# Block sums of the up-projection weights, made in the prompt's pass and stored for the sample's

## The chip, the core and the metric

The kernel runs on one core of a Trainium2 chip. The metric is device time in microseconds (us); lower is better. The core's engines run side by side, each with its own queue of instructions: TensorE (PE, matmuls; PEld its weight loads), VectorE (DVE), ScalarE (ACT), GpSimd (POOL) and SyncE (SP, which issues most DMAs). GpSimd issues DMAs too, from a queue of its own. Operands lie in SBUF, an on-chip memory of 128 partitions; matmuls accumulate into PSUM, which has eight banks of 128 x 512 fp32.

## The reference

One layer of an encoder is applied with the same weights to a prompt of 512 tokens and then to a sample of 1024 tokens, all in fp32, model width 1024. A retention branch and a latent-attention branch are merged by gates and projected (`w_out`); then follows the gated MLP that the change is about:

```python
    x = x + merged @ w_out[l]
    h = rms_norm(x, g_ffn[l])
    u = depthwise_conv3(h @ w_up[l], conv_w[l], conv_b[l])
    x = x + (jax.nn.silu(u[..., :D_FF]) * u[..., D_FF:]) @ w_down[l]
```

`w_up` is 1024 x 5632 and `w_down` 2816 x 1024. `depthwise_conv3` mixes each token with its two neighbours, channel by channel.

## The kernel before

**Precision.** An fp32 product is made of three products of a shorter type: `split` writes `hi` (a rounded copy, ScalarE, L121) and `lo` (source minus `hi`, VectorE, L122), and the matmuls hi x hi, hi x lo and lo x hi add up in PSUM. Every weight block is loaded (`raw`, 512 KB), split into `whi` and `wlo`, and used. Tensors are kept transposed, channels on partitions and tokens along the row, in 128-channel pieces.

**Order.** The layer function does the prompt, then the sample. A scheduler with a timeline of its own lays the instructions of each engine into one queue, so an engine does them in that order and waits at the first that isn't ready. Tiles come from pools; a tile tag with n buffers makes the next use wait until the n-th last one is read out.

**Prompt MLP** (L520 to L637). `psw` is the projection by `w_out`; its result is added to x, scaled to h2 and split (`h2h`, `h2l`), and x goes to DRAM. `do_up(j)` makes the 128 channels j of both halves of the up projection (`psu`, 48 matmuls), scales by the norm (`rb2`), applies the convolution (one ScalarE pass L579, two VectorE passes L580 and L581 for a half), silu and the gate product, and splits the result (`gh`, `gl`). `do_down(i)` takes two such blocks through `w_down`: eight matmul groups `psd` of 6, each added to y (L614). Up and down blocks alternate, and pieces of the sample's input preparation (`prep`: x loads, `hh`/`hl` splits, squares) run in between, with the norm of the sample's input (`rstd_n`, `spread`) at the end. The sample's projections `psc` follow.

**Sample MLP** (`mlp_by_seven`, L643 on). The up projection is done by a scheme of seven products on 2 x 2 blocks instead of eight. Its data units are b11, t2, t3 (pool "far") and t1, b21, t4, b22 (pool "near"), made of sums of quarters of h2. Its weight units, for each of 22 pairs j of column blocks, are the quarters a11, a12, a22 and the sums s1 = a21 + a22, s2 = s1 - a11, s3 = a11 - a21, s4 = a12 - s2. `up_weights(j)` loads the two 512 KB blocks of the pair, makes the four sums on GpSimd (L689 to L694) and splits the seven 512-wide units. `up_pair(j)` runs the seven products (12 matmuls each) in the order b11, t2, t3, t1, b21, t4, b22 into the tiles `psxw` (X and W), `psy`, `psz`, then combines them (L786 to L793, three of the sums on GpSimd), scales by `rb`, convolves (L797 to L799) and stores the gated result to DRAM (`gact`, L803). The near units are built at the start of the stage from VectorE splits and GpSimd sums. The norm of h2 (`pn_n`, `psr_n`) is computed in pair 0, after all its products. The down projection (`psd`, L836) follows as a stage of its own.

Of the kernel before, what the change touches and what calls it, by code (L numbers as in the profile page):

```python
# [45 lines left out]
def encoder(ctx: ExitStack, tc: tile.TileContext, a: dict):  # L46
# [226 lines left out]
    def layer(L, yT, following=None):  # L273
# [19 lines left out]
        def dense(ps, w, xh, xl):  # L293
            kn = len(xh)
            for k in range(kn):
                for pi, (wk, x) in enumerate(((w[k][0], xh), (w[k][0], xl), (w[k][1], xh))):
                    for h in range(nh):
                        nc.tensor.matmul(  # L298
                            ps[h] if isinstance(ps, list) else ps[:, hs[h]], wk, x[k][:, hs[h]],
                            start=(k == 0 and pi == 0), stop=(k == kn - 1 and pi == 2))  # L300

# [18 lines left out]
        for j in range(6):  # L320
# [177 lines left out]

        mgp, mgst = open_pool(f"md{sq}")
# [20 lines left out]
        hp2, h2st = open_pool(f"h2{sq}", 1, "right")  # L520
        h2h, h2l = new_split(hp2, KD, "h2")
        rb2 = hp2.tile([P, s], F32, tag="rb2", name=f"rb2{sq}")
        xp, xst = open_pool(f"xo{sq}", 2, "right")
        acc = xp.tile([P, s], F32, tag="acc", name=f"acc2{sq}", bufs=1)
        for m in range(KD):
            w = load_k(a["wout"][m], KD, P)
            x = xp.tile([P, s], F32, tag="x", name=f"xo{m}{sq}")
            nc.sync.dma_start(x, xT[m])
            ps = acc_tile(f"psw{m}{sq}")
            dense(ps, w, mh, ml)  # L530
            g = gffn[:, m:m + 1]
            nc.vector.tensor_tensor(x, ps[:, :s], x, op=ALU.add)
# [811 lines left out]
```

## Time and profile before

| | |
|---|---|
| Runs | 2975.9, 2975.2 and 3527.12 us; median 2975.9 |
| Profiled execution | 2975.95 us; its span 2974.2 us |
| TensorE busy in the span | 2905.5 us (98%) |
| VectorE, ScalarE, GpSimd busy | 67%, 45%, 20% |
| DMA | 323.89 MB, mean 109 GB/s |
| Prompt's `psw`, MLP and the sample's `psc` and first norm | 537.3 to 1028.1 us of the span |
| Sample's up projection | 2246.9 to 2728.7 us of the span |

A row of the profile names line, engine and operation, then what is written and what is read (`out<-in`, buffer numbers left out), the shape and the count; behind the bar stand busy time and mean ns of one. PEclk is the clock granted to TensorE as a share of full speed. "Idle before, releaser" tells how long the engine stood still ahead of an instruction and what ended the wait. The busy time of neighbouring instructions of one engine can overlap a little: a matmul of 512 columns is listed with some 0.39 us, while its successor starts 0.23 us after it, so the pace of TensorE is read from starts (in the chain of waits: so many matmuls in so many us) and not from its mean duration.

### The profile page before, as it was taken

The page shows a single profiled execution, that of the slowest core. Times are in us where ns is not written, and L with a number is a line of the kernel's source. Part 1 is how long each engine was busy: PE and PEld are TensorE (multiplying, and loading weights), DVE is VectorE, ACT ScalarE, POOL GpSimd, SP SyncE. Part 2 cuts the span into 40 slices and gives each one's busy share as a digit, 9 for nine tenths or more (in the row PEclk, how much of TensorE's full clock was granted, in tenths as well). Part 3 has the DMA queues.
Part 4 walks back from the last instruction along what each step waited for, and adds up shares of the span by engine and source line. Part 5 has one row for each costly group of instructions (what it writes and reads, how often), then busy time and mean ns, then how long its engine had stood idle before and what let it go on. Part 6 is the DMA issues. An engine that isn't in the chain of part 4 may idle for free.

```text
span 2974.2 us, 41678 instructions
## 1 busy us (share of the span) xinstructions
PE 2905.5 (98%) x15720; PEld 2499.0 (84%) x15720; DVE 1992.4 (67%) x3602; ACT 1340.4 (45%) x2634; POOL 592.6 (20%) x540
## 2 busy tenths in 40 slices
PE   8999999999999999999999999999998999999999
PEld 7998887878887899999888888888886777777887
DVE  6766786578666446765347888872458999988343
ACT  5554674344332234444246677651234444434222
POOL 1011220000000001001122122100025667764000
PEclk9999999999999999999999999999998999999999
DMA  6225444543232411112332222324431212224463
GB/s 192 84 92 180 141 143 148 181 142 121 92 99 89 156 44 44 54 45 77 114 108 73 73 78 79 121 83 169 143 134 50 85 64 85 71 78 163 144 204 113
DMA packets 127801, 323.89 MB, mean 109 GB/s; under 512 B 13040, under 2 KB 45680, under 8 KB 127600
## 3 DMA queue, kind: packets, MB, share of 16 engines
q1 hardware_dynamic: 78192, 232.60, 24.2%
q0 software_dynamic: 49408, 88.62, 9.7%
q8 instruction: 124, 2.03, 0.3%
q14 instruction: 77, 0.63, 0.1%
HBM read 257.73 MB, written 63.44 MB: 108 GB/s over the span
## 4 chain that ended last, share of the span: by engine, by line
PE 81%; DVE 12%; ACT 2%; issue 2%; POOL 2%; DMA 2%; SPq 0%; DVEq 0%; POOLq 0%; ACTq 0%
PE psr L890 14%; PE psd L836 8%; PE S L1185 6%; PE pv L1218 4%; DVE wu L122 3%; PE pq L1131 2%; PE pkv L1062 2%; PE psw L298 2%; DVE t L798 2%; DVE t L799 2%; PE pt L1206 2%; PE psxw L761 2%; PE po L1010 2%; POOL u L791 1%; PE psz L761 1%
## 5 line engine op out<-in xcount | busy, mean ns | idle before, releaser
L121 ACT ACTIVATE whi<-raw 128x1024 fp32r<-128x1024 f32 (+3 forms) x274 | 263.9, 966 | 670.4 <-PE psd L836 144.6
L122 DVE TENSOR_TENSOR wlo<-raw,whi 128x1024 fp32r<-128x1024 f32 (+2 forms) x272 | 301.4, 1110 | 224.5 <-ACT whi L121 224.4
L122 DVE TENSOR_TENSOR ptl<-pt,pth 128x512 fp32r<-128x512 f32 x160 | 107.3, 685 | 26.2 <-ACT pth L121 24.9
L836 PE MATMUL psd<-gh,whi 128*128 128x512 f32 x352 | 109.4, 394 | 4.1 <-ACT gh L121 4.1
L1187 DVE TENSOR_REDUCE mx<-S 128x1 f32<-128x1024 f32 (+1 forms) x96 | 99.9, 1041 | 14.7 <-PE S L1185 13.6
L836 PE MATMUL psd<-gl,whi 128*128 128x512 f32 x352 | 108.8, 389 | 0.0
L836 PE MATMUL psd<-gh,wlo 128*128 128x512 f32 x352 | 108.5, 389 | 0.0
L1190 ACT ACTIVATE pe<-S,mx,qsc 128x1024 f32<-128x1024 f32 (+1 forms) x96 | 102.4, 1067 | 6.6 <-DVE mx L1188 6.5
L121 ACT ACTIVATE pth<-pt 128x512 fp32r<-128x512 f32 x160 | 91.2, 599 | 29.8 <-PE pt L1206 28.0
L798 DVE SCALAR_TENSOR_TENSOR t<-u,consts,t 128x1023 f32<-128x1023 f32 x44 | 78.4, 1795 | 25.7 <-ACT t L797 25.1
L121 ACT ACTIVATE wu<-s 128x512 fp32r<-128x512 f32 x88 | 53.4, 626 | 82.2 <-POOL s L690 63.0
L1206 PE MATMUL pt<-ident,pe 128*128 128x128 f32 x640 | 89.0, 273 | 0.5 <-DVE pe L1192 0.2
L797 ACT ACTIVATE t<-u,consts 128x1024 f32<-128x1024 f32 x44 | 53.6, 1244 | 76.7 <-POOL u L791 59.6
L122 DVE TENSOR_TENSOR wu<-s,wu 128x512 fp32r<-128x512 f32 x88 | 82.9, 964 | 1.7 <-ACT wu L121 1.5
L1131 PE MATMUL pq<-whi,qc 128*128 128x384 f32 x288 | 83.7, 346 | 0.0
L122 DVE TENSOR_TENSOR wu<-rawu,wu 128x512 fp32r<-128x512 f32 x66 | 80.0, 1213 | 4.1 <-ACT wu L121 4.0
L1017 POOL TENSOR_TENSOR rsd<-rsd,mhalf 128x2 f32<-128x2 f32 x24 | 20.0, 832 | 314.2 <-DVE rsd L1016 314.2
L836 PEld LDWEIGHTS psd<-gh,whi 128*128 128x128 f32 x352 | 67.0, 191 | 18.5 <-ACT gh L121 4.5
L1206 PEld LDWEIGHTS pt<-ident,pe 128*128 128x128 f32 x640 | 73.9, 140 | 7.2 <-DVE ptl L122 1.3
L799 DVE SCALAR_TENSOR_TENSOR t<-u,consts,t 128x1023 f32<-128x1023 f32 x44 | 78.1, 1777 | 0.0
L836 PEld LDWEIGHTS psd<-gl,whi 128*128 128x128 f32 x352 | 66.1, 188 | 13.7
L836 PEld LDWEIGHTS psd<-gh,wlo 128*128 128x128 f32 x352 | 66.1, 188 | 13.7
(7524 smaller groups left out, 9908.1 us busy)
## 6 DMA issues: line engine op xcount, KB each, us to landing
raw<-wr SPq DMA_DIRECT2D x48, 512.0 KB, 3.5
raw<-wup SPq DMA_DIRECT2D x44, 512.0 KB, 3.5
rawu<-wup SPq DMA_DIRECT2D x44, 512.0 KB, 3.5
gr<-gact SPq DMA_DIRECT2D x44, 512.0 KB, 3.5
raw<-wg SPq DMA_DIRECT2D x32, 512.0 KB, 4.0
qc<-c0s POOLq DMA_DIRECT2D x16, 768.0 KB, 5.6
raw<-wdn SPq DMA_DIRECT2D x22, 512.0 KB, 3.6
gact<-t POOLq DMA_DIRECT2D x22, 512.0 KB, 3.1
```

Source lines behind the costliest of these rows:

```text
L121: first = nc.scalar.activation(hi, src, AF.Copy)
L122: nc.vector.tensor_tensor(lo, src, hi.bitcast(F32), op=ALU.subtract)
L798: nc.vector.scalar_tensor_tensor(t[:, 1:], u[i][:, :s - 1], convw[:, 0, c:c + 1], t[:, 1:], op0=ALU.mult, op1=ALU.add)
L799: nc.vector.scalar_tensor_tensor(t[:, :s - 1], u[i][:, 1:], convw[:, 2, c:c + 1], t[:, :s - 1], op0=ALU.mult, op1=ALU.add)
L836: nc.tensor.matmul(acc_[i][h], w[:, ms], x[:, t_of[h]], start=(k == 0 and pi == 0), stop=(k == NF - 1 and pi == 2))
L890: nc.tensor.matmul(ps[:, t], x[k][:, tk], w, start=(k == 0 and pi == 0), stop=(k == KD - 1 and pi == 2))
L1131: nc.tensor.matmul(ps[:, :384], x[:, k, tk], w, start=(k == 0 and pi == 0), stop=(k == 2 and pi == 2))
L1185: nc.tensor.matmul(S[:, ks], l_, r_, start=(i == 0), stop=(i == 4))
L1187: nc.vector.reduce_max(mx[:, 0:1], S[:, :s], axis=AX.X)
L1190: nc.scalar.activation(pe, S[:, :s], AF.Exp, scale=Q["sc"][:, 0, e, j:j + 1], bias=mx[:, 1:2], accum_out=mx[:, 2:3])
L1206: nc.tensor.transpose(pt[:, c], pe[:, kk * P:(kk + 1) * P], ident)
L1218: nc.tensor.matmul(po[:, :256], w[:, kk, e], x[:, kk % 4], start=(kk == 0 and pi == 0), stop=(kk == ns - 1 and pi == 2))
```

## The change

In the prompt, the MLP becomes `mlp_in_two`. Its first phase does all 22 pairs of up blocks. Each pair has a double PSUM tile (`psu`), its raw weights come from a pool of their own with four buffers, and the gated results stay in SBUF (22 tiles). For each pair VectorE also makes the four weight sums from the raw tiles and GpSimd's queue stores them to the DRAM tensor `upsum` (88 stores of 256 KB). The second phase runs the 22 steps of the down projection into eight PSUM banks at once, with the splits `gh`, `gl` made step by step, and y added once at the end. The sample's preparation runs in the second phase, but the norm of its input is computed in its `psc` projection, as the prompt's was already. The pool of h2 is opened before that of the merge operands: h2 moves from byte 194528 of each partition to byte 60032, where the merge operands were, and these to 94848.

In the sample, `up_weights(j, part)` loads the seven weight units as 256 KB halves, three from `wup` and four from `upsum`, two to a raw tile, and splits them 1024 wide (the seventh 512 wide). All sums that GpSimd made in this MLP are made by VectorE. `up_first` (products b11, t2, t3) of pairs 0 and 1 both come before `up_second(0)`, and the norm of h2 comes behind pair 1's first products. In the down projection, the two double PSUM tiles serve the first and fourth accumulators.

```diff
-        else:
-            rstd_n(L["rn"], acc, D, f"n1{sq}")
-            spread(L["rb"], L["rn"], xp, f"n1{sq}")
...
+        if nh == 1:
+            h2 = open_pool(f"h2{sq}")
         mgp, mgst = open_pool(f"md{sq}")
...
+    up_d = dpool.tile([NF, 4, P, 512], F32, tag="upsum", name="upsum")
+    def mlp_in_two(xT, yT, x2_d, mh, ml, mgst, dense, h2, following):
...
+        rawp, rawst = open_pool("ra5", 4, "right")
...
+        up, ust = open_pool("up5", 2)
+        gs = []
+        for j in range(NF):
+            both = ps_a(f"psu{j}p")
+            raws, ts_ = [], []
+            for mi, c in enumerate((j, j + NF)):
+                raw = rawp.tile([P, WB], F32, tag="raw", name=f"rawu{c}p")
+                hi = wpool.tile([P, WB], F32R, tag="whi", name=f"wuh{c}p")
+                lo = wpool.tile([P, WB], F32R, tag="wlo", name=f"wul{c}p")
+                nc.sync.dma_start(raw, a["wup"][c])
+                split(raw, hi, lo)
+                raws += [raw[:, :H], raw[:, H:]]
...
+            for mi, c in enumerate((j, j + NF)):
+                u = up.tile([P, s], F32, tag="u", name=f"u{c}p")
+                t = gp.tile([P, s], F32, tag=f"g{j}", name=f"t{c}p") if mi else up.tile([P, s], F32, tag="t", name=f"t{c}p")
+                nc.vector.tensor_tensor(u, both[:, mi * H:(mi + 1) * H], rb2, op=ALU.mult)
...
+            a11, a12, a21, a22 = raws
+            s1, s2, s3, s4 = [up.tile([P, H], F32, tag=f"s{i}", name=f"sw{i}_{j}", bufs=1) for i in range(4)]
+            nc.vector.tensor_tensor(s1, a21, a22, op=ALU.add)
+            nc.vector.tensor_tensor(s3, a11, a21, op=ALU.subtract)
+            nc.vector.tensor_tensor(s2, s1, a11, op=ALU.subtract)
+            nc.vector.tensor_tensor(s4, a12, s2, op=ALU.subtract)
+            for i, t in enumerate((s1, s3, s2, s4)):
+                nc.gpsimd.dma_start(up_d[j, i], t)
...
+        acc_ = [ps_b("psd0p"), ps_b("psd1p"), ps_p("psd2p"), ps_o("psd3p")]
+        for i in range(2):
+            both = ps_a(f"psd{4 + 2 * i}p")
+            acc_ += [both[:, :H], both[:, H:]]
+        for k in range(NF):
+            wh, wl = load_w(a["wdn"][k], WB)
...
+            split(gs[k], gh, gl)
+            for m in range(KD):
+                ms = slice(m * P, (m + 1) * P)
+                for pi, (w, x) in enumerate(((wh, gh), (wh, gl), (wl, gh))):
+                    nc.tensor.matmul(acc_[m], w[:, ms], x, start=(k == 0 and pi == 0), stop=(k == NF - 1 and pi == 2))
+            if k % 2:
+                run(steps, 1)
+        for m in range(KD):
+            nc.vector.tensor_tensor(y[m], acc_[m], y[m], op=ALU.add)
...
-        def up_weights(j):
-            raw = []
-            for c in (j, j + NF):
-                r = wpool.tile([P, WB], F32, tag="raw", name=f"rawu{c}", bufs=2)
-                nc.sync.dma_start(r, a["wup"][c])
...
-            nc.gpsimd.tensor_tensor(s1, a21, a22, op=ALU.add)
-            nc.gpsimd.tensor_tensor(s2, s1, a11, op=ALU.subtract)
...
+        def up_weights(j, part):
+            ab = (a["wup"][j], a["wup"][j + NF])
+            src = ((("b11", ab[0][:, :H]), ("t2", up_d[j, 2])), (("t3", up_d[j, 1]), ("t1", up_d[j, 0])),
+                   (("b21", ab[0][:, H:]), ("t4", ab[1][:, H:])), (("b22", up_d[j, 3]),))
+            for group in src[2 * part:2 * part + 2]:
...
+                raw = wpool.tile([P, WB], F32, tag="raw", name=f"rawu{n}", bufs=2)
...
+                for q, (_, ap) in enumerate(group):
+                    nc.sync.dma_start(raw[:, q * H:(q + 1) * H], ap)
+                c0 = slice(0, H * len(group))
+                split(raw[:, c0], hi[:, c0], lo[:, c0])
...
-                nc.gpsimd.tensor_tensor(b12, b12, b11, op=ALU.subtract)
+                nc.vector.tensor_tensor(b12, b12, b11, op=ALU.subtract)
...
-            nc.gpsimd.tensor_tensor(p7, p7, p5, op=ALU.add)
-            nc.gpsimd.tensor_tensor(u[1][:, t_of[1]], p7, u2, op=ALU.add)
+            nc.vector.tensor_tensor(p7, p7, p5, op=ALU.add)
+            nc.vector.tensor_tensor(u[1][:, t_of[1]], p7, u2, op=ALU.add)
...
-            nc.gpsimd.tensor_tensor(u[1], u[1], rb, op=ALU.mult)
+            nc.vector.tensor_tensor(u[1], u[1], rb, op=ALU.mult)
...
+        up_first(0)
+        up_weights(0, 1)
+        end = up_first(1)
+        rb2 = [up.tile([P, s], F32, tag="rb2", name="rb2_7")]
+        with tc.issue_after(end.ins):
+            rstd_n(rn2, acc, D, "n2_7")
+            spread(rb2[0], rn2, up, "n2_7")
         for j in range(NF):
-            nxt = up_weights(j + 1) if j + 1 < NF else None
-            up_pair(j, ready)
-            ready = nxt
+            if j > 1:
+                up_first(j)
+            if j:
+                up_weights(j, 1)
+            if 0 < j < NF - 1:
+                up_weights(j + 1, 0)
+            up_second(j)
```

What this does to the queues is shown at three places, in the order of the program.

SyncE's queue in the prompt, at the merge projection. `mlld` are pieces of the attention branch for it, `mhg` and `mhr` its gate operands, `raw` from `wmo` its weights, `rawu` up-projection weights; the number behind a name is the block. Before:

```order
L441 DMA mlld0p<-mlap 128x512
L441 DMA mlld1p<-mlap 128x512
L441 DMA mlld2p<-mlap 128x512
L133 DMA raw_6326<-wmo 128x1024
L441 DMA mlld3p<-mlap 128x512
L441 DMA mlld4p<-mlap 128x512
L133 DMA raw_6365<-wmo 128x1024
L441 DMA mlld5p<-mlap 128x512
L441 DMA mlld6p<-mlap 128x512
L441 DMA mlld7p<-mlap 128x512
```

And after:

```order
L439 DMA mlld0p<-mlap 128x512
L439 DMA mlld1p<-mlap 128x512
L565 DMA rawu0p<-wup 128x1024
L565 DMA rawu22p<-wup 128x1024
L565 DMA rawu1p<-wup 128x1024
L565 DMA rawu23p<-wup 128x1024
L439 DMA mlld2p<-mlap 128x512
L439 DMA mlld3p<-mlap 128x512
L133 DMA raw_6330<-wmo 128x1024
L509 DMA mhg00p<-gate1p 128x512
L510 DMA mhr00p<-mrgp 128x512
L509 DMA mhg10p<-gate1p 128x512
```

Four loads of up-projection weights now stand between `mlld1p` and `mlld2p`.

VectorE's queue in the prompt's up projection, before, around block 13 (`t130p` and `t131p` are its two halves):

```order
L122 TENSOR_TENSOR wlo_8541<-raw_8539,whi_8540 128x1024
L122 TENSOR_TENSOR gl12p<-t121p,gh12p 128x512
L578 TENSOR_TENSOR u130p<-psu13p,rb2p 128x512
L122 TENSOR_TENSOR wlo_8583<-raw_8581,whi_8582 128x1024
L580 SCALAR_TENSOR_TENSOR t130p<-u130p,consts,t130p 128x511
L581 SCALAR_TENSOR_TENSOR t130p<-u130p,consts,t130p 128x511
L578 TENSOR_TENSOR u131p<-psu13p,rb2p 128x512
L122 TENSOR_TENSOR wlo_8589<-raw_8587,whi_8588 128x1024
L578 TENSOR_TENSOR u140p<-psu14p,rb2p 128x512
L122 TENSOR_TENSOR wlo_8666<-raw_8664,whi_8665 128x1024
L580 SCALAR_TENSOR_TENSOR t131p<-u131p,consts,t131p 128x511
L580 SCALAR_TENSOR_TENSOR t140p<-u140p,consts,t140p 128x511
```

After, most of one period in the later half of the phase; `sw_19` are the four weight sums of pair 19, `wul18p` the `lo` of pair 18's first raw tile, `u16p` and `u38p` the two halves of pair 16:

```order
L590 TENSOR_TENSOR sw_19_8583<-rawu41p 128x512
L591 TENSOR_TENSOR sw_19_8585<-rawu19p,rawu41p 128x512
L586 TENSOR_TENSOR t37p<-t15p,t37p 128x512
L592 TENSOR_TENSOR sw_19_8584<-sw_19_8583,rawu19p 128x512
L122 TENSOR_TENSOR wul18p<-rawu18p,wuh18p 128x1024
L593 TENSOR_TENSOR sw_19_8586<-rawu19p,sw_19_8584 128x512
L580 TENSOR_TENSOR u16p<-psu16p,rb2p 128x512
L580 TENSOR_TENSOR u38p<-psu16p,rb2p 128x512
L122 TENSOR_TENSOR wul40p<-rawu40p,wuh40p 128x1024
L582 SCALAR_TENSOR_TENSOR t16p<-u16p,consts,t16p 128x511
L582 SCALAR_TENSOR_TENSOR t38p<-u38p,consts,t38p 128x511
L583 SCALAR_TENSOR_TENSOR t16p<-u16p,consts,t16p 128x511
```

A period has 13 instructions, the last being a fourth convolution pass. The sums of a pair come three pairs ahead of its convolution and before the `lo` split of the same raw tiles; the `gl` splits and y additions are gone from here.

TensorE's queue where the sample's up projection reaches its first near product. `psxw`, `psy`, `psz` are the output tiles (before, `psxw` 23357 is pair 0's and 23534 pair 1's; after, those of pair 1 are 23473 and 23475), `b11`, `t3` far units, `t1` a near one, `pn_n` the norm. Before:

```order
L761 MATMUL psxw_7_23534<-b11h_7_23122,wu_23334 128x512
L761 MATMUL psxw_7_23534<-b11l_7_23123,wu_23334 128x512
L761 MATMUL psxw_7_23534<-b11h_7_23122,wu_23334 128x512
L248 MATMUL pn_n_7_23451<-ones,acc_7_22635 128x1 x8
L761 MATMUL psxw_7_23357<-t1h_7_23243,wu_23205 128x512
L761 MATMUL psxw_7_23357<-t1l_7_23244,wu_23205 128x512
L761 MATMUL psxw_7_23357<-t1h_7_23243,wu_23205 128x512
L761 MATMUL psxw_7_23357<-t1h_7_23248,wu_23205 128x512
```

After:

```order
L741 MATMUL psz_7_23475<-t3l_7_23153,wuh_23326 128x512
L741 MATMUL psz_7_23475<-t3h_7_23152,wul_23327 128x512
L741 MATMUL psz_7_23475<-t3h_7_23308,wuh_23326 128x512
L741 MATMUL psz_7_23475<-t3l_7_23309,wuh_23326 128x512
L741 MATMUL psz_7_23475<-t3h_7_23308,wul_23327 128x512
L741 MATMUL psxw_7_23473<-t1h_7_23336,wuh_23326 128x512
L741 MATMUL psxw_7_23473<-t1l_7_23337,wuh_23326 128x512
```

Before, 48 matmuls stand ahead of the first with `t1` (pair 0's b11, t2 and t3, pair 1's b11) and the norm is right in front of it; now 72 do, and the first `t1` product is pair 1's, with the norm 36 matmuls further on.

More of the change, by code (lines that the diff above doesn't have):

```diff
@@ L584, in do_up @@
             nc.vector.tensor_tensor(ts_[1], ts_[0], ts_[1], op=ALU.mult)
-            pool = gx[0] if j == NF - 1 else gp
-            hi = pool.tile([P, s], F32R, tag="gh", name=f"gh{j}{sq}")
-            lo = pool.tile([P, s], F32R, tag="gl", name=f"gl{j}{sq}")
-            split(ts_[1], hi, lo)
-            g[j] = (hi, lo)
-        def do_down(i):
-            ws = [load_w(a["wdn"][2 * i + k], WB) for k in range(2)]
-            pairs = [g.pop(2 * i), g.pop(2 * i + 1)]
+            gs.append(ts_[1])
@@ L594, in do_down @@
+        for i in range(2):
[3 more added lines that the diff above has]
+            wh, wl = load_w(a["wdn"][k], WB)
+            gh = gq.tile([P, s], F32R, tag="gh", name=f"gh{k}p")
+            gl = gq.tile([P, s], F32R, tag="gl", name=f"gl{k}p")
+            split(gs[k], gh, gl)
             for m in range(KD):
                 ms = slice(m * P, (m + 1) * P)
[L596 to L600 removed]
@@ L601, in do_down @@
-                for k in range(2):
-                    xh, xl = pairs[k]
-                    wh, wl = ws[k]
-                    for pi, (w, x) in enumerate(((wh, xh), (wh, xl), (wl, xh))):
-                        for h in range(nh):
-                            nc.tensor.matmul(pss[h], w[:, ms], x[:, hs[h]],
-                                             start=(k == 0 and pi == 0), stop=(k == 1 and pi == 2))
-                if i == 0:
-                    src = xr.tile([P, nxt["s"] if nxt else s], F32, tag="x", name=f"xr{m}{sq}")[:, :s]
-                    nc.sync.dma_start(src, x2_d[m])
-                else:
-                    src = y[m]
@@ L751, in mlp_by_seven, with product, keep, up_first @@
         up, ust = open_pool("up7", 1, "right")
-        def up_pair(j, w):
+        live = {}
+        def product(u, j, out, first):
+            w = uw.pop((u, j))
+            ops = [(w[k][wi_], unit[u, k][xi]) for k in range(KH) for wi_, xi in ((0, 0), (0, 1), (1, 0))]
+            for i, (l_, r_) in enumerate(ops):
+                mm = nc.tensor.matmul(out, l_, r_, start=(first and i == 0), stop=(i == len(ops) - 1), skip_group_check=True)
+            return mm
+        def keep(src, name, j):
+            t = st(f"{name}{j}_7") if j == 1 else up.tile([P, H], F32, tag=name, name=f"{name}{j}_7")
+            nc.scalar.activation(t, src, AF.Copy)
+            return t
+        def up_first(j):
             xw = ps_a(f"psxw{j}_7")
```

198 lines of the change are left out of this document (72 added, 126 removed).

## The prediction

> **What bounds the kernel now.** I read the page first, for the engines over the span.
>
> ```profile
> PE 2905.5 (98%) x15720; PEld 2499.0 (84%) x15720; DVE 1992.4 (67%) x3602; ACT 1340.4 (45%) x2634; POOL 592.6 (20%) x540
> DVE  6766786578666446765347888872458999988343
> POOL 1011220000000001001122122100025667764000
> PEclk9999999999999999999999999999998999999999
> ```
>
> TensorE is busy 98% of the span, so a change can win only where it waits, where its clock is down, or where a matmul itself takes longer than it need. Slices 31 to 37, the sample's up projection, are the one stretch with VectorE at 0.9, GpSimd at 0.6 and a dent in the clock. Busy time by windows, for the two stretches that the change rewrites and pieces of them:
>
> ```profile
> core 0: us, PE busy (x) PEld busy (x) DVE busy (x) ACT busy (x) POOL busy (x), PEclk, DMA share, GB/s
> 481.00:581.00 100.00, 99.52 (x433) 81.30 (x434) 54.99 (x71) 35.85 (x49) 5.40 (x10) 1.00 0.62 198
> 537.30:1028.10 490.80, 485.64 (x2096) 391.21 (x2095) 316.65 (x416) 180.40 (x215) 13.55 (x16) 0.99 0.38 123
> 945.00:1032.00 87.00, 85.61 (x396) 70.60 (x395) 35.54 (x50) 22.33 (x24) 7.28 (x7) 0.96 0.43 146
> 2246.90:2728.70 481.80, 444.58 (x1870) 357.47 (x1868) 439.22 (x397) 209.38 (x308) 320.60 (x176) 0.96 0.23 79
> 2424.40:2427.80 3.40, 3.33 (x8) 2.66 (x9) 3.29 (x6) 2.75 (x5) 0.00 (x0) 0.50 0.00 0
> 2430.00:2480.00 50.00, 50.00 (x219) 40.82 (x218) 46.42 (x40) 20.62 (x31) 37.02 (x21) 1.00 0.27 93
> ```
>
> The third row runs from the prompt's `psw` to the sample's first retention matmul, the fifth is the sample's up projection (22 pairs of 84 matmuls, 1848 in all). The last row is that stage when nothing waits: 50.00/219 = 0.2283 us a matmul, 0.2283 x 1848 = 421.9 us, with some 1.6 us for the norm's small matmuls 423.5. The stage takes 481.8, so 58.3 us are over: 481.80 - 444.58 = 37.2 of idle, and 21.1 in slow matmuls. The waits say whom TensorE waited for:
>
> ```profile
> PE pn_n L248 <- DVE acc L729: 10.7, 1, 10.7
> PE psxw L761 <- DVE wu L122: 10.3, 5, 2.1
> PE psd L836 <- ACT gh L121: 4.1, 1, 4.1
> PE psy L761 <- ACT wu L121: 4.1, 3, 2.3
> ```
>
> Mostly VectorE, or ScalarE's splits fed through it. The row 2424.40:2427.80 lies right behind such a wait of 2.06 us: granted clock 0.50 for 3.4 us, so a short wait costs about 1.7 us more than itself. Groups of VectorE and GpSimd in 2290:2720 (mean ns behind the comma), and then single instructions of the timeline (start, duration):
>
> ```profile
> L122 DVE TENSOR_TENSOR wu<-rawu,wu 128x512 fp32r<-128x512 f32 x60 | 76.0, 1266 | 0.1
> L798 DVE SCALAR_TENSOR_TENSOR t<-u,consts,t 128x1023 f32<-128x1023 f32 x42 | 75.9, 1820 | 23.9 <-ACT t L797 23.3
> L802 DVE TENSOR_TENSOR t<-t,t 128x1024 f32<-128x1024 f32 x20 | 44.0, 2200 | 0.0
> L789 DVE TENSOR_TENSOR u<-psxw,rb 128x512 f32<-128x512 f32 x21 | 14.3, 681 | 4.9 <-PE psxw L761 4.9
> L791 POOL TENSOR_TENSOR u<-u,rb 128x1024 f32<-128x1024 f32 x21 | 56.9, 2711 | 18.0 <-DVE u L790 9.5 <-ACT rb L271 8.4
> ```
>
> ```profile
> 2298.89 2.27 POOL L787 TENSOR_TENSOR p<-p,p 128x512 f32<-128x512 f32 x1
> 2297.70 2.31 DVE L798 SCALAR_TENSOR_TENSOR t<-u,consts,t 128x1023 f32<-128x1023 f32 x1
> 2309.10 0.68 DVE L122 TENSOR_TENSOR wu<-s,wu 128x512 fp32r<-128x512 f32 x1
> 2309.70 0.68 DVE L790 TENSOR_TENSOR u<-psz,u 128x512 f32<-128x512 f32 x1
> 2314.56 1.28 DVE L798 SCALAR_TENSOR_TENSOR t<-u,consts,t 128x1023 f32<-128x1023 f32 x1 [0.16 <-ACT t L797]
> 2315.49 1.52 POOL L689 TENSOR_TENSOR s<-rawu 128x512 f32<-128x512 f32 x1 [2.25 <-DMA rawu<-wup]
> ```
>
> The same instruction, L798, takes 2.31 us under a GpSimd sum and 1.28 where GpSimd waits for a DMA. A sum that reads PSUM (L789) keeps its 0.68. VectorE is full here because half its instructions are stretched by GpSimd's, and two that follow each other start 0.60 apart for 0.68 of duration.
>
> **Sample's up projection.** GpSimd loses all seven kinds of sums there. Four (the weight sums) are gone, the others go to VectorE. Its work for a pair, by the code and the unstretched durations: three 1024-wide `lo` subtracts at 1.22 (row below) and one of 512 at 0.68, seven 512-wide combinations at 0.68, the 1024-wide u x rb and gate product at 1.22, four STT at 1.28: 4.34 + 4.76 + 2.44 + 5.12 = 16.7; 17 instructions that overlap by 0.08 each: 15.3 us, against 84 x 0.2283 = 19.2 of TensorE. Before it was 439.22/22 = 20.0, more than TensorE. So I cost the moved sums at nothing, covered by 3.9 us a pair; without that cover they are 0.60 x 2 + 1.14 = 2.3 a pair, 51 us.
>
> Start: 72 matmuls (pairs 0 and 1) come before the first near product, 16.4 us, where 48 do now; the first nine near ones add 2.1. VectorE's row to the last `t1` part is, by the order, 20 ops of 0.60, two 1024-wide splits or acc sums at 1.14 and two halves of `xo` at 0.60, and one more split: 12.0 + 2.3 + 1.2 + 0.6 = 16.1, from 1.5 us after the last `psw`: ready at 17.6 where 18.5 is needed. The 10.7 us goes, and the norm, now behind the near products, waits for nothing. Next in line is the reload of weight pieces: two 256 KB loads where one of 512 KB stood, some 2 us of slack a pair by the order. Left: 2 us at the end, where the last pair's activations still precede `gh` (4.1 now, with stretched instructions in the chain), 2 of small waits, 2 of slow clock. 423.5 + 6 = 429.5; **gain 52.3**.
>
> **Prompt.** The chain of waits gives the matmuls' pace (start, duration, count):
>
> ```profile
> 575.61 5.44 PE psw7p L298 x24
> 691.34 5.60 PE psu7p L298 x24
> 706.03 1.40 PE psd240p L606 x6
> ```
>
> ```profile
> L122 DVE TENSOR_TENSOR wlo<-raw,whi 128x1024 fp32r<-128x1024 f32 x63 | 76.3, 1219 | 15.0 <-ACT whi L121 14.9
> L268 DVE TENSOR_TENSOR dg_n2p<-ident,rhl_n2p 128x512 fp32r<-128x512 f32 x2 | 1.3, 684 | 0.0
> L580 DVE SCALAR_TENSOR_TENSOR t90p<-u90p,consts,t90p 128x511 f32<-128x511 f32 x1 | 0.8, 753 | 0.9 <-ACT t90p L579 0.9
> L578 DVE TENSOR_TENSOR u90p<-psu9p,rb2p 128x512 f32<-128x512 f32 x1 | 0.7, 692 | 0.4 <-PE psu9p L298 0.4
> ```
>
> ```profile
> raw<-wup SPq DMA_DIRECT2D x44, 512.0 KB, 3.5
> gact<-t POOLq DMA_DIRECT2D x22, 512.0 KB, 3.1
> c1p<-ch4p POOLq DMA_DIRECT2D x1, 512.0 KB, 4.9
> ```
>
> `psu` runs at 5.60 for 24, `psw` at 5.44. Their shapes agree; what differs in the built program is the SBUF place of the moving operand, h2 high (byte 194528 of a partition on), mg low (60032 on). The change puts h2 at 60032. If the pace goes with the place: 44 x 0.16 = 7.0 gained. Bounds: 0 (it doesn't) and 7.0; I take 7.0, since only these two rows bear on it. The down operands stay in the middle, at `psd`'s pace.
>
> Idle is 490.80 - 485.64 = 5.2 us, in the interleaving that goes, and the clock of 0.96 over 87 us costs 3.5. Two phases bring one stop of their own, the first `c` matmul behind the eight last additions (about 1.5 us, and 1.7 by clock). Gain 7.0 + 5.2 + 3.5 - 3.2 = 12.5. The sums' price: VectorE's cycle for a pair of 48 matmuls (2 x 5.44 = 10.88 us) is 2 x 1.22 + 5 x 0.684 + 2 x 0.69 + 4 x 0.753 = 10.25, less 13 x 0.08: 9.2. I take nothing, covered by 1.7 us. But the raw tile, of four, is now held until `s4` and the `lo` split: by the order its reload has only the four STT (2.7 us) as cover for a load of 3.5. That makes a cycle of 10.0 to 10.3, still under 10.88; at 4.9 a load, 11.4, or 11 us over 22 pairs, of which the double PSUM tile hides about 9 once.
>
> Ahead of it, SP's queue has four loads of `rawu` (2 MB) set before the merge operands `mlld2p` on. At the 198 GB/s of the row 481:581 they are 10.6 us of traffic, in a window whose TensorE idles 0.5 of 100. Bounds 0 and 10; I take 1, the nearer row being the window that has swallowed such loads already.
>
> The 88 stores to DRAM (23 MB) and their issue on GpSimd's queue I cost at nothing: GpSimd has no other work there and nobody waits but the single `sw` tiles. Three other edits (order of the down accumulators, norm of the sample's input moved behind its third `c` block, `y` through PSUM) are within the 1.5 above.
>
> **Sum.** Profiled time of its own 2975.95, which is the median of the runs: 2975.95 - 52.3 - 12.5 + 1.0 = **2912 us**, own range 2898 to 2920. The bound of 2%, about what a measurement of this kernel can tell from no change, is 2916.4 and 3035.4.
>
> **The clock's rule.** The Trainium skill ("TensorE: Matmul & The Clock Gate", Part 1) says that the gate throttles after an idle window of about 3.4 us, and that such windows run free. By that alone only two waits of this stage (10.7 and 4.1) throttle, and most of the 21.1 us would have another cause and stay. The row 2424.40:2427.80, 0.50 after a wait of 2.06, speaks against it; the rule's case is rival C.
>
> **Rivals.**
> A. **The prompt's up phase is bound by VectorE and the reload.** Against: 9.2 of 10.88 by durations. For: a raw tile's reload has 2.7 us of cover. A cycle of 11.4 to 12.4 (loads of 4.9, or stores of 3.1 in line, 4 x 3.1) loses 11 to 33: 2923 to 2945. Chance 0.14.
> B. **Weights come late in the sample.** Two tiles of raw, loads from two tensors: if 2 us stay on each group's first use, 0.5 a pair with its clock loss on every second: 22 x 0.5 + 11 x 1 = 22: about 2934. For: 10 of the 37.2 idle sits on `wu` now. Against: those came with stretched splits. Chance 0.13.
> C. **The slow clock stays** but for what two long waits explain (2 x 1.7): 21.1 - 3.4 - 2 = 15.7 us back: 2928. Chance 0.06.
> D. **Slower: the stores hold VectorE.** Place: `sw` tiles, one of each, whose next write waits for its store. If GpSimd's queue writes its four stores one after the other while VectorE is 85% busy, the cycle is four times a store. At the row's 4.9, 19.6 against 10.88, 22 x 8.7 = 192: 3104. No change at 10.88 + 64/22 = 13.8, a store of 3.45; 2% slower from 16.5, a store of 4.1. For: nothing else queues so many. Against: `gact` leaves on the same queue in 3.1 for twice the bytes with VectorE at 0.9. The Trainium skill ("SBUF — State Buffer", the trap "DVE blocks DMA") warns of GpSimd-queue transfers starved of descriptors under VectorE; it names other operations than these subtracts, and no run here shows it yet. Chance 0.06.
> E. **It doesn't do what it says.** VectorE's long rows come of its own load, not GpSimd's: 15.3 x 1820/1280 = 21.8 a pair, 479 for the stage: no gain there, 2964. Against: 1.28 beside 2.31. Chance 0.04.
>
> **Chances.** Forecast 0.57, A 0.14, B 0.13, C 0.06, D 0.06, E 0.04. The forecast's range lies four fifths under 2916.4: 0.46; a further 0.04 from A and B, where one comes with more of the other gain. Faster 0.50; slower 0.06 (D); within 2% 0.44. Range 2898 to 2945 holds forecast, A, B and C, less their ends.
>
> **What would show it.** GpSimd without sums in the sample's up stage, `lo` splits of 1024 at 1.2 and STT at 1.3, TensorE idle under 10 us, clock 0.99: the main step right. `psu` at 5.44 for 24: the place. A prompt `psu` that starts later than 10.9 us after the one before, waiting for `wul` or `u`: A; VectorE waiting for a DMA `upsum`: D; `psxw` or `psy` waiting for splits fed by `rawu` loads: B. Wrong would be this if the sample's stage came out above 445 us or the prompt's above 490.

## The result, and the profile after

The changed kernel takes 2910.89 us (median of 4 runs, 2910.28 to 2911.35); the ratio to the kernel before is 0.9778, 95% interval 0.9759 to 0.9797. The forecast was 2912, range 2898 to 2945. That is 2.2% faster, just past the bound of 2%. The slow run of 3527 us of the kernel before is not in the ratio.

The page of the changed kernel, the rows that answer to those of before:

```profile
PE 2876.3 (99%) x15720; PEld 2487.7 (86%) x15720; DVE 1911.4 (66%) x3626; ACT 1334.2 (46%) x2568; POOL 307.4 (11%) x466
DVE  6766786688873346666437888874346888887343
POOL 1011221021100100001112222100000000000000
PEclk9999999999999999999999999999999999999999
```

GpSimd has left the sample's up projection (the last quarter of its row), VectorE's load there is down to 0.8, the dent in the clock is gone. The windows of the two rewritten stretches, cut at the same events as before (first `psw` of the prompt to the sample's first retention matmul; the sample's up projection), in the columns of the prediction's table of windows:

```profile
539.10:1016.00 476.90, 474.47 (x2094) 389.30 (x2093) 319.56 (x426) 179.38 (x215) 64.14 (x112) 1.00 0.51 173
2235.90:2663.40 427.50, 426.38 (x1869) 349.30 (x1867) 359.72 (x402) 203.25 (x244) 13.41 (x23) 1.00 0.38 125
```

Measured between the first matmuls of the tiles that begin each stretch, the spans of the two profiled executions compare like this:

| Stretch | before, us | after, us | difference | forecast |
|---|---|---|---|---|
| prompt's merge projection (`psmo`) | 44.8 | 46.4 | +1.6 | +1.0 |
| prompt's `psw`, MLP, `psc` | 490.7 | 476.8 | -13.9 | -12.5 |
| sample: retention to `psw` | 1219.1 | 1219.9 | +0.9 | 0 |
| sample's up projection | 481.6 | 427.6 | -54.1 | -52.3 |
| sample's down projection, to the end | 245.5 | 245.1 | -0.4 | 0 |

What TensorE still waits for in the sample's up stage, and its longest wait in 481:1020 of the prompt (two more are 0.5 us each):

```profile
PE psd L831 <- ACT gh L121: 1.1, 1, 1.1
PE psd L831 <- DVE gl L122: 0.5, 1, 0.5
```

```profile
PE psu2p L295 <- DVE u22p L580: 2.0, 1, 2.0
```

VectorE's groups in 2290:2660, with GpSimd quiet:

```profile
L122 DVE TENSOR_TENSOR wul<-rawu,wuh 128x1024 fp32r<-128x1024 f32 x56 | 68.6, 1224 | 25.3 <-ACT wuh L121 25.2
L783 DVE SCALAR_TENSOR_TENSOR t<-u,consts,t 128x1023 f32<-128x1023 f32 x40 | 51.1, 1280 | 21.2 <-ACT t L782 21.1
L776 DVE TENSOR_TENSOR u<-u,rb 128x1024 f32<-128x1024 f32 x21 | 25.7, 1224 | 0.6
```

The convolution pass is at 1.28 where it was 1.82, the product with `rb` takes VectorE 1.22 where it took GpSimd 2.71.

### The profile page after: what moved, and what is told of

Read it like the earlier page. It is cut to its first block, busy times and chain, and to the rows that moved or that the text cites. A ratio compares the mean times of both kernels' runs of the same rounds, so it can differ in the third digit from the quotient of the medians.

```text
span 2908.5 us, 41912 instructions
## 1 busy us (share of the span) xinstructions
PE 2876.3 (99%) x15720; PEld 2487.7 (86%) x15720; DVE 1911.4 (66%) x3626; ACT 1334.2 (46%) x2568; POOL 307.4 (11%) x466
## 4 chain that ended last, share of the span: by engine, by line
PE 94%; DMA 2%; DVE 2%; issue 1%; ACT 1%; POOL 0%; SPq 0%; DVEq 0%; POOLq 0%; ACTq 0%
PE psr L885 14%; PE psxw L741 8%; PE psd L831 8%; PE S L1180 6%; PE psz L741 4%; PE pv L1213 4%; PE psw L295 3%; PE pq L1126 2%; PE pkv L1057 2%; PE psy L741 2%; PE pt L1201 2%; PE po L1005 2%; PE psd6p L621 1%; PE psd4p L621 1%; PE psd3p L621 1%
## 5 line engine op out<-in xcount | busy, mean ns | idle before, releaser
L121 ACT ACTIVATE whi<-raw 128x1024 fp32r<-128x1024 f32 (+3 forms) x230 | 218.0, 949 | 602.9 <-PE psd L831 144.9
L122 DVE TENSOR_TENSOR wlo<-raw,whi 128x1024 fp32r<-128x1024 f32 (+3 forms) x228 | 247.4, 1085 | 259.1 <-ACT whi L121 259.1
L121 ACT ACTIVATE wuh<-rawu 128x1024 fp32r<-128x1024 f32 x88 | 83.8, 953 | 145.3 <-PE psxw L741 79.4
L122 DVE TENSOR_TENSOR wul<-rawu,wuh 128x1024 fp32r<-128x1024 f32 x88 | 95.6, 1088 | 28.9 <-ACT wuh L121 28.9
L1057 PE MATMUL pkv<-whi,kc 128*128 128x512 f32 x192 | 68.9, 400 | 2.7 <-DMA kc<-c1s 1.7
L783 DVE SCALAR_TENSOR_TENSOR t<-u,consts,t 128x1023 f32<-128x1023 f32 x44 | 56.2, 1280 | 22.4 <-ACT t L782 22.3
L1187 DVE TENSOR_SCALAR pe<-pe,mx 128x1024 f32<-128x1024 f32 (+1 forms) x96 | 64.0, 667 | 2.1
L595 POOL DMA_DIRECT2D upsum<-sw x88 | 47.5, 540 | 161.1 <-DVE sw L590 98.0
L122 DVE TENSOR_TENSOR gl<-gr,gh 128x1024 fp32r<-128x1024 f32 x44 | 53.8, 1224 | 13.9 <-ACT gh L121 13.9
```

Of the source, the lines that this page charges most:

```text
L121: first = nc.scalar.activation(hi, src, AF.Copy)
L122: nc.vector.tensor_tensor(lo, src, hi.bitcast(F32), op=ALU.subtract)
L1057: nc.tensor.matmul(ps, x[:, k, tk], w, start=(k == 0 and pi == 0), stop=(k == 1 and pi == 2))
```

## The experiments

Times of the kernel before in the same sessions were 2976.0 to 2978.3 us. Stage lengths are from the traces, cut as in the table above. The kernels for which one time is given without a ratio or a range were executed once. Runs of one kernel here differ by 1 to 7 us, so those kernels are judged by what their traces show within a stage and not by a few us of the whole time.

**Is it GpSimd?** The kernel before, with only the engine of the sample MLP's sums exchanged:

```diff
-            nc.gpsimd.tensor_tensor(s1, a21, a22, op=ALU.add)
+            nc.vector.tensor_tensor(s1, a21, a22, op=ALU.add)
...
-            nc.gpsimd.tensor_tensor(p7, p7, p5, op=ALU.add)
+            nc.vector.tensor_tensor(p7, p7, p5, op=ALU.add)
```

and so with all eleven of its GpSimd sums.

> The kernel before, with nothing changed but the engine of the sample MLP's sums: all of GpSimd's (four weight sums a pair, three combinations a pair, those of the near units) run on VectorE. Theory 1 (VectorE is stretched by GpSimd's sums): VectorE's work for a pair becomes seven splits and eleven 512-wide sums at 0.60, two 1024-wide at 1.14, four passes at 1.2 = 17.9 us, under TensorE's 19.2, so most of the 37 us of idle and 21 us of slow matmuls in the sample's up stage go: stage 435 to 450 us (481.8 before, 427.6 changed), whole kernel 2930 to 2945. Rival (VectorE is simply full): 20.0 us a pair plus seven sums more, 24 to 25 us a pair, stage 540, whole kernel 3030.

Measured: 2932.97 us, ratio 0.985 (0.983 to 0.9869); the up stage 439.8 us. This kernel's groups in 2290:2680, and what TensorE waits for in the stage:

```profile
L799 DVE SCALAR_TENSOR_TENSOR t<-u,consts,t 128x1023 f32<-128x1023 f32 x42 | 53.6, 1277 | 0.0
L122 DVE TENSOR_TENSOR wu<-s,wu 128x512 fp32r<-128x512 f32 x80 | 52.2, 684 | 0.0
```

```profile
PE pn_n L248 <- DVE acc L729: 6.6, 1, 6.6
PE psd L836 <- ACT gh L121: 2.2, 1, 2.2
PE psxw L761 <- ACT p L765: 1.3, 1, 1.3
```

VectorE got seven sums a pair more to do and its work fits, because each instruction is as short as when alone. 41.8 of the 54.1 us come with this exchange of engines, though the whole kernel stays inside the bound of 2%. The weight sums need not be stored ahead for that.

**The same from the other side.** The changed kernel, with GpSimd sums that nobody waits for:

```diff
-            nc.gpsimd.dma_start(g_d[j], ts_[1])
+            out = nc.gpsimd.dma_start(g_d[j], ts_[1])
+            with tc.issue_after(out.ins):
+                for k in range(2 * KH if j > 1 else 0):
+                    nc.gpsimd.tensor_tensor(st(f"idle{k}_{j}"), unit["b11", k % KH][0].bitcast(F32), unit["b11", k % KH][1].bitcast(F32), op=ALU.add)
```

> The changed kernel, with eight added GpSimd sums of 512 in each pair of the sample's up stage from pair 2 on, of data that nobody waits for and into tiles that nobody reads (work added, nothing left out). Theory 1 (GpSimd's sums stretch VectorE's instructions with two SBUF inputs): GpSimd busy some 15 us a pair again, VectorE's splits and convolution passes back at 1.7 to 2.3 us, VectorE 20 to 22 us a pair against 19.2 of TensorE; stage 427.6 to 460 or 490. Rival (VectorE's long rows came of its own load or of the order): stage unchanged within 2 us.

Measured: 3081.72 us, the up stage 596.5. The rival is out, but the forecast of my own theory was far too low, and the trace says why. Its VectorE and GpSimd groups in 2400:2790, and VectorE then GpSimd on the timeline:

```profile
L776 DVE TENSOR_TENSOR u<-u,rb 128x1024 f32<-128x1024 f32 x15 | 152.6, 10172 | 0.5
L122 DVE TENSOR_TENSOR wul<-rawu,wuh 128x1024 fp32r<-128x1024 f32 x43 | 52.5, 1221 | 5.8 <-ACT wuh L121 5.8
```

```profile
L791 POOL TENSOR_TENSOR idle<-b11h,b11l 128x512 f32<-128x512 f32 x113 | 141.6, 1286 | 0.3
```

```profile
2524.96 0.68 DVE L775 TENSOR_TENSOR u<-psz,u 128x512 f32<-128x512 f32 x1
2525.68 10.77 DVE L776 TENSOR_TENSOR u<-u,rb 128x1024 f32<-128x1024 f32 x1
```

```profile
2525.33 10.03 POOL L791 TENSOR_TENSOR idle<-b11h,b11l 128x512 f32<-128x512 f32 x8
```

GpSimd's sums run back to back at 1.29 us, and the one VectorE instruction that comes while they run stands still for the whole row of eight (8 x 1.29 = 10.3 us by their mean, 10.03 by the timeline; it is listed with 10.17). GpSimd's row ends at 2535.4, VectorE's instruction at 2536.5, its own 1.1 us later. Everything else of VectorE is at full speed. So it is not a slowing of both, spread over the time, but one engine shut out until the other lets go. The Trainium skill ("SBUF — State Buffer", Who interferes with whom) describes the shared port pair as an exclusive lock in which the loser fully blocks; these rows agree, and add that a row of GpSimd instructions without waits between them did not let VectorE in. Nine us are lost in each pair, more than the 3.9 that VectorE had to spare, so VectorE sets the pace: once the sums run, the `gact` stores of neighbouring pairs are issued 26.9 us apart, against 19.3 in the changed kernel. Over the 17 pairs at this pace that makes some 130 of the 169 us; the second wait below, at the stage's end, makes most of the rest. TensorE's two longest waits are

```profile
PE psxw L741 <- ACT wuh L121: 84.8, 15, 12.6
PE psd L834 <- ACT gh L121: 33.7, 1, 33.7
```

That GpSimd's sums hold up VectorE was right and the price was not: I had taken the stretch of before, 0.6 to 1 us an instruction, where GpSimd had waits between its sums.

**How much the three combinations alone cost.** The changed kernel with them back on GpSimd:

```diff
-            nc.vector.tensor_tensor(p7, p7, p5, op=ALU.add)
-            nc.vector.tensor_tensor(u[1][:, t_of[1]], p7, u2, op=ALU.add)
+            nc.gpsimd.tensor_tensor(p7, p7, p5, op=ALU.add)
+            nc.gpsimd.tensor_tensor(u[1][:, t_of[1]], p7, u2, op=ALU.add)
...
-            nc.vector.tensor_tensor(u[1], u[1], rb, op=ALU.mult)
+            nc.gpsimd.tensor_tensor(u[1], u[1], rb, op=ALU.mult)
```

> The changed kernel, with the three combinations a pair of the sample's up stage (p7 + p5, + u2, u x rb) back on GpSimd; the weight sums stay stored. Theory 1 (stretching by GpSimd): GpSimd works some 6 us a pair, about as long VectorE's two-input instructions are stretched by 0.6 to 1 us each; VectorE 13.0 us of work plus 4 to 6 of stretch, 17 to 19 a pair against TensorE's 19.2, with the order laid out for other times: the stage 428 to 440 (427.6 changed). If the combinations alone had been the trouble of before: 460 and more. If only the weight sums were: 428.

Measured: 2919.06 us, the stage 434.4: 6.9 us more. VectorE in 2280:2660 and TensorE's waits in the stage:

```profile
L122 DVE TENSOR_TENSOR wul<-rawu,wuh 128x1024 fp32r<-128x1024 f32 x57 | 87.3, 1531 | 3.6 <-ACT wuh L121 3.3
L787 DVE TENSOR_TENSOR t<-t,t 128x1024 f32<-128x1024 f32 x20 | 43.6, 2180 | 0.3
```

```profile
PE psd L831 <- ACT gh L121: 3.4, 1, 3.4
PE psxw L741 <- DVE wul L122: 1.8, 1, 1.8
```

The product L787 is at 2.18 again, the splits at 1.53, but VectorE has time for it in the steady pairs. TensorE's waits show at the ends of the stage, 5.2 us against 1.6. So the combinations alone were not the trouble of before. No kernel put the weight sums alone back on GpSimd, so whether they would have been enough, or only both groups together, is not shown.

**The early products.** Pair 1's first products and the norm where they were before:

```diff
         up_first(0)
         up_weights(0, 1)
-        end = up_first(1)
...
         for j in range(NF):
-            if j > 1:
+            if j:
                 up_first(j)
```

> The changed kernel, with pair 1's first products and the norm put back in the order of before (48 matmuls ahead of the first near product instead of 72, the norm behind pair 0's products). By the prediction's count the last t1 part is ready 15 to 17.6 us after psw and needed after 13.0: a wait of 2 to 4.6 us and some 2 to 3 of slow clock, stage 427.6 to 432 to 436. Rival (the early order does nothing once GpSimd is out): 428.

Measured: 2919.64 us, the stage 433.3, 5.7 us more; one wait of 4.1 us (for ScalarE's copy `p`) at the start and slow clock behind it (0.96 in 2239:2280):

```profile
PE psxw L741 <- ACT p L746: 4.1, 1, 4.1
```

The size is as counted; the engine that was waited for is not the one of the count (VectorE's last `t1` part), so the count was right only as to how much work the early products must cover.

**The prompt's cover.** Each weight sum made twice in VectorE's row:

```diff
-            nc.vector.tensor_tensor(s1, a21, a22, op=ALU.add)
-            nc.vector.tensor_tensor(s3, a11, a21, op=ALU.subtract)
+            for _ in range(2):
+                nc.vector.tensor_tensor(s1, a21, a22, op=ALU.add)
+                nc.vector.tensor_tensor(s3, a11, a21, op=ALU.subtract)
```

and likewise s2 and s4.

> The changed kernel, with each of the four weight sums of a prompt pair made twice in VectorE's row (88 instructions of 0.60 us more, the second overwriting the first with the same values). By the prediction's budget VectorE goes from 9.2 to 11.6 us a pair and the reload of a raw tile waits longer, against TensorE's 10.88: 0.7 to 1.8 us a pair, 16 to 40 less the 9 that the double PSUM tile hides: prompt's stage 476.8 to 484 or 507. Rival (the sums were never near the limit): 476.8, no change.

Measured: 2932.69 us, the prompt's stage 499.5, 22.7 us more. Window 600:800 of this kernel, and its longest wait in the up phase (there are others of about 2 us):

```profile
600.00:800.00 200.00, 186.78 (x791) 150.30 (x790) 189.20 (x278) 71.94 (x87) 32.21 (x60) 0.97 0.48 158
```

```profile
PE psu10p L295 <- ACT wuh10p L121: 2.5, 1, 2.5
```

2.4 us more a pair stop TensorE at `wuh`, the split of a raw tile that came late. The sums are free only because they fit: 1.7 us a pair were left by the budget, and less than 2.4 were there.

**The place of h2.** The prediction took 7.0 us from the low place of h2. Four kernels tell place from alignment. In the changed kernel the weight tiles start at multiples of 128 bytes of a partition, h2 at 60032, also a multiple of 128; before, h2 started at 194528, which is 96 over. First, h2 on the high side (149472, 96 over a multiple):

```diff
-        if nh == 1:
-            h2 = open_pool(f"h2{sq}")
...
         gp, gst = open_pool("g5", 1, "right")
+        hp2, h2st = open_pool("h2p", 1, "right")
```

> The changed kernel, with the pool of h2 opened later and on the other side, so that h2 lies at byte 149472 of a partition on instead of 60032; the order of the work is the same. Place theory: the prompt's up matmuls go from 5.44 to 5.60 for 24, 44 x 0.16 = 7.0 us more in the prompt's stage (476.8 to 484). Rival (the pace came with the interleaved work of before): still 5.44, no difference.

Measured: 2916.23 us, prompt's stage 484.6. Then all weights moved instead:

```diff
-    wpool = ctx.enter_context(tc.tile_pool(name="wpool", bufs=WBUFS))
+    wpool = ctx.enter_context(tc.tile_pool(name="wpool", bufs=WBUFS, side="right"))
```

> The changed kernel, with the pool of weight tiles (raw, hi, lo) at the top end of SBUF, 188384 on, instead of 19072 to 60032, so that everything else slides down by 40960 bytes; the order is the same. Place theory, absolute (a moving operand that lies high is slow, wherever the weights are): the prompt's down projection (its moving operand now at 92832) goes from 0.234 to 0.227 a matmul, 528 x 0.0067 = 3.5 us less, the sample's score matmuls (keys and queries now below 131968 in part) a few us less, the rest unchanged: 2900 to 2907. Place theory, relative (slow when moving operand and weights lie in different halves): all the fast projections become slow, 20 to 60 us more. No place theory: 2911.

Measured: 2950.57 us, ratio 0.9907 (0.9891 to 0.9924) to the kernel before, 40 us more than the changed kernel. Projections that had run at 5.44 for 24 ran at 5.6, and the sample's merge projection, slow until then, ran at full pace. The chain of waits for its group 3, changed kernel first, then the one with the weights high:

```profile
2092.96 11.20 PE psmo3s L295 x48
```

```profile
2118.61 10.88 PE psmo3s L295 x48
```

Low or high is therefore not the cause by itself; the place relative to the weights' is, or something finer. In this kernel the weights start 96 over a multiple of 128 (188384), and so does `ml` (122848), while h2 and the merge operands are at multiples. That led to a new theory: a matmul is slow where the places of moving operand and weights differ modulo 128 bytes. Two kernels complete the square, h2 high at a multiple (96 unused bytes above it, 149376), and h2 low off a multiple (96 bytes below it, 60128; the merge operands move with it, so `psw` is slower there too). The edit of the first:

```diff
+        pad, padst = open_pool("pad5", 1, "right")
+        nc.vector.memset(pad.tile([P, 24], F32, tag="pad", name="pad5"), 0.0)
         gp, gst = open_pool("g5", 1, "right")
```

> The kernel with h2 on the high side, moved down by 96 bytes to byte 149376, a multiple of 128 as the weight tiles' places are. Place theory (high is slow): the prompt's up matmuls at 5.60 for 24, prompt's stage 484 as with h2 at 149472. Alignment theory: 5.44, prompt's stage 477.

> The changed kernel with 96 unused bytes ahead of h2 on the low side: h2 at 60128 and the merge operands at 94944, neither a multiple of 128. Place theory: up matmuls at 5.44 for 24 and psw too, stage 477. Alignment theory: psu and psw of the prompt at 5.60, 52 x 0.16 = 8.3 more, stage 485.

Measured: 2909.69 us with prompt's stage 476.5, and 2916.84 us with 484.1. The chain of waits of the four, one pair of the prompt's up phase (48 matmuls) each: changed (low, multiple); high, off; high, multiple; low, off:

```profile
620.14 10.88 PE psu3p L295 x48
```

```profile
620.41 11.20 PE psu3p L295 x48
```

```profile
618.23 10.88 PE psu3p L295 x48
```

```profile
621.20 11.20 PE psu3p L295 x48
```

The offset decides and the place does nothing: 22 x 0.32 = 7.0 us, the term of the prediction, from another cause than the one it named. These four hold the offsets 0 and 96 only; they do not show that the period is 128.

**All moving operands on multiples of 128.** The changed kernel with unused bytes in four pools, for `ml`, the far units, the prompt's `gh`/`gl` and the score operands:

```diff
+            pad, padst = open_pool(f"pad{sq}", 1, "right")
+            nc.vector.memset(pad.tile([P, 24], F32, tag="pad", name=f"padm{sq}"), 0.0)
             mp, mst = open_pool(f"ml{sq}", 1, "right")
...
-        rn2 = stp.tile([P, s // P], F32, tag="rn2", name="rn2_7", bufs=1)
+        rn2 = stp.tile([P, 24], F32, tag="rn2", name="rn2_7", bufs=1)[:, :s // P]
...
+        if not L["lead"]:
+            nc.vector.memset(xp.tile([P, 24], F32, tag="pad", name=f"padx{sq}", bufs=1), 0.0)
...
-                ss = sp.tile([P, 2], F32, tag="kss", name=f"kss{pr}{t}")
+                ss = sp.tile([P, 16], F32, tag="kss", name=f"kss{pr}{t}")[:, :2]
...
-            mx = sp.tile([P, 4], F32, tag="mx", name=f"mx{hd}{t}")
+            mx = sp.tile([P, 16], F32, tag="mx", name=f"mx{hd}{t}")[:, :4]
```

> The changed kernel, with a few unused bytes put into four pools (96 under the merge operands ml, 64 in st7, 96 in the pool of the sample's squares, 56 and 48 in two small tiles of the attention pool), so that every tile read as moving operand by ml, far, prompt down and score matmuls starts at a byte that is a multiple of 128, as the weights do; nothing else. Alignment theory (a matmul is slow where moving operand and weights differ modulo 128 bytes, whatever half they lie in): merge projections 0.233 to 0.227 (192 + 384 of them, 3.6 us), prompt's down projection 0.234 to 0.227 (528, 3.5 us), far units 0.2305 to 0.227 (792, 2.8 us), scores 0.233 to 0.227 (some 800, up to 4.8 us): 10 to 15 us less, 2896 to 2901. Half theory (the place as such, low or high, together with the weights' place): nothing changes, 2911.

Measured: 2905.57 us (5 runs, 2901.18 to 2906.86). The sample's merge projection runs at full pace and the up stage takes 423.0 us, 4.6 less. Chain of waits of the changed kernel for a pair of the up stage (b22 with b11, then pieces of t2 and t3), and then that of the aligned one, with the merge group of above ahead:

```profile
2314.69 5.49 PE psxw L741 x24
2320.18 1.62 PE psy L741 x7
2321.80 2.29 PE psz L741 x10
```

```profile
2090.06 10.88 PE psmo3s L297 x48
...
2309.33 5.44 PE psxw L748 x24
2314.77 1.59 PE psy L748 x7
2316.36 2.27 PE psz L748 x10
```

The matmuls of these rows go from between 0.229 and 0.231 to 0.227.

The prompt's down projection stayed at its pace (window 850:940, changed and then aligned):

```profile
850.00:940.00 90.00, 90.00 (x387) 72.29 (x386) 39.08 (x43) 33.49 (x41) 0.00 (x0) 1.00 0.37 121
```

```profile
850.00:940.00 90.00, 90.00 (x387) 72.44 (x386) 39.52 (x45) 32.93 (x39) 0.00 (x0) 1.00 0.34 115
```

387 matmuls touch the 90 us both times, a pace of 0.233. The score matmuls gained little too (the whole stretch from retention to `psw` is 2.6 us shorter, of which the merge projection is 2.6). The gain is 5 us where 10 to 15 were expected; the 3.5 and up to 4.8 expected of these two are what is missing.

The places in the built programs suggest why. Every stream that ran at 0.2267 has moving operand and weights at the same byte modulo 256 too. The unused bytes were counted for 128, and in the aligned kernel the prompt's `gh` starts at 133888 and its weights at 27264: both are multiples of 128, and they are 128 apart modulo 256. So are half of the score matmuls. And one product got worse: in `pkv` the weight tile is the moving operand (27264 in both kernels) and `kc` the stationary one, at 177024 in the changed kernel, equal modulo 256, and at 176896 in the aligned one, 128 apart. Twelve of them in a row, changed and then aligned:

```profile
1497.88 2.72 PE pkv L1057 x12
```

```profile
1495.96 2.79 PE pkv L1064 x12
```

That is 0.2267 and 0.2325 each, though both kernels have the two operands equal modulo 128. Over all `pkv` matmuls that start right behind another the mean is 0.2304 and 0.2325, in the second profile of each kernel 0.2303 and 0.2325. So equality modulo 128 is not enough, and a period of 256 fits `pkv`, the down projection and the fast streams alike; the score matmuls mix both cases within a row and do not tell. No kernel was run with the down projection equal modulo 256, so there the period is argued and not shown. The changed and the aligned kernel timed side by side in one session:

> The changed kernel as it is, timed beside the aligned one: 2911 within 3 us by either theory.

> The changed kernel with the unused bytes in four pools again, timed beside the changed one. By the first look's stages (merge 1.1 and 2.6 us, far units 4.6, middle 2.6 less): 5 to 10 us under it.

Measured: 2909.71 us for the changed kernel (2908.13 to 2911.71, ratio to before 0.9778, 0.9765 to 0.9792) and 2904.03 for the aligned one (2902.50 to 2907.74, ratio 0.976, 0.9746 to 0.9773). The intervals of the ratios just overlap, the times of the runs do not. The up stage gains 4.5 us again (427.5 and 423.0), but the stretch from retention to `psw` is not shorter this time (1219.5 and 1219.6). In this second profile of the aligned kernel the prompt's stage was 480.1 us against 476.7 in the first, and the wait at `psu2p` 3.5 us against 2.4. That wait is what is next in line, and its cause stands in the chain of the changed kernel at the start of the up phase:

```profile
589.61 5.12 DMA upsum<-sw
...
602.11 4.73 DMA upsum<-sw
...
606.94 0.69 DVE sw L593
607.63 0.60 DVE u0p L580
608.23 0.61 DVE u22p L580
```

Two stores of 5.1 and 4.7 us, on the chain because the single `sw` tiles must be stored before the next pair's sums; `u0p` and `u22p`, which free the PSUM tile, stand behind those sums in VectorE's row.

## Why the prediction was right

**The sample's gain (52.3 forecast, 54.1 measured).** The step that GpSimd stretches VectorE held from both sides: take GpSimd's sums away from the kernel before and 41.8 us go, add idle ones to the changed kernel and 169 us come. Of the rest, the early products are worth 5.7. What remains, some 7 us if these add up, is in the wider splits and the stored sums, and was not measured by itself. The residual of 6 us over the floor of 423.5 was put too high: 427.6 were measured, and of the 4.1 only 1.6 are waits. About as much is the floor itself, a misreading of the prediction: its 219 matmuls in 50 us include those cut by the edges, and from start to start a matmul of the changed kernel's stage takes 0.2292 us, not 0.2283, which is 1848 x 0.0009 = 1.7. The far units' offset is in that pace before and after the change; with it mended the stage takes 423.0. The price that the prediction gave for lost cover, 2.3 us a pair, was never due.

**The prompt (12.5 forecast, 13.9 measured).** The term for h2, 7.0, came out by size, from the offset and not from the place: the sentence "if the pace goes with the place" named the wrong cause, as the four kernels show. The two rows on which it stood could not have told one from the other. That the low byte 60032 also has the weights' offset was luck: at 60128, as low, the 7.0 us would not have come. The stop behind the last additions, 3.2 with its clock, did not come; instead 2.0 us are lost at `psu2p`, where the prediction had nothing. The sums cost nothing, as forecast, and with double the sums 22.7 us came, inside the 16 to 40 less 9 that the budget gave.

**The merge projection (+1.0 forecast, +1.6 measured).** The window takes the four loads set ahead of `mlld2p` nearly whole. That the 1.6 is their doing was not shown, since no kernel left them out.

**The rivals.** A did not decide, but VectorE does wait for late `rawu` loads and the room is under 2.4 us a pair. B fell: `wu` and `wuh` no longer appear among the waits of the stage. C fell: the stage runs at a clock of 1.00 and its slow matmuls went with the short waits. By the rule of the Trainium skill ("TensorE: Matmul & The Clock Gate", Part 1), taken as a bound of 3.4 us on the wait, they should have stayed; the measurement differs. That page's free-running window would fit a wait that sometimes costs the clock and sometimes does not. The trace agrees as far as that: a wait of 2.0 us at `psu2p` left the clock of 600:640 at 1.00 in the changed kernel, and one of 2.1 at the same place brought it to 0.96 in the kernel with h2 high:

```profile
600.00:640.00 40.00, 37.99 (x168) 31.12 (x167) 37.95 (x55) 18.74 (x24) 10.84 (x21) 1.00 0.70 243
```

```profile
600.00:640.00 40.00, 37.86 (x156) 30.10 (x155) 36.27 (x52) 16.51 (x21) 10.23 (x19) 0.96 0.63 223
```

D was true for the first pairs (stores of about 5 us hold VectorE), and false for the phase: its median store landed in 2.8 us, below the 3.45 from which D would have decided. The row held against D, that `gact` leaves in 3.1 with VectorE busy, was the right one to go by. The Trainium skill ("SBUF — State Buffer", the trap "DVE blocks DMA") warns of starvation under VectorE; it did not show under these subtracts:

```profile
upsum<-sw POOLq DMA_DIRECT2D x88, 256.0 KB, 2.8
```

E fell with the first two experiments.

## What to carry to other kernels

Before sums are moved off a full VectorE to an idle GpSimd, look at one instruction in the timeline twice, with GpSimd at work and without: here 1.28 against 2.31 us said that GpSimd's help cost more than it gave, and an exchange of engines in one function was worth three quarters of the gain of its stage. A margin of under 2 us a pair can hide real work, but only the pairs in the middle of a phase have it; the first and the last pair have to be checked by themselves. When a matmul's pace differs between two places, compare the starting bytes of both operands, modulo 256 as well as 128, before believing in a place.

## What the runs showed of the hardware

A 512-column matmul started every 0.2267 us where moving operand and weights start at the same byte modulo 256, and every 0.233 where they were 32, 96 or 128 apart; with 64 apart (the far units before they were aligned) it was between, 0.229 to 0.231. The fast pace held with both at multiples of 128 for the prompt's and the sample's merge, `psw` and up projections, and with both 96 over for the merge projections (weights at the high end). Equality modulo 128 alone did not bring it: `pkv` ran at 0.2325 so, and the prompt's down projection at 0.233. That the period is 256 rests on kernels that were built for 128.

A VectorE product with two inputs in SBUF that met eight GpSimd sums in a row took 10.2 us instead of 1.2; the sums themselves were not slowed (1.29 us).

A wait of about 2 us was followed by half clock in some cases and not in others, within one program too: in the kernel before, two waits for `wu` of 2.06 us each end at 2424.5 and 2486.4 us of the span, and the clock of the next 3.4 us is 0.50 behind the first (1.7 us lost) and 1.00 behind the second.
